# Dealing two small experts' 23 steps out by weight instead of one behind every four units

## The chip, the cores and the metric

The kernel runs on one core of a Trainium2 chip. The metric is the device time of one execution in microseconds (us). TensorE (PE) multiplies, VectorE (DVE), ScalarE (ACT) and GpSimd (POOL) do elementwise work, and SyncE (SP) issues most of the transfers from HBM. Weights come from HBM into on-chip buffers, and matmul results land in eight PSUM banks.

## The reference, cut to what matters

Two trunk layers run on 384 tokens (128 context tokens and 256 latent tokens). Layer 0 ends in a dense SwiGLU, layer 1 in a mixture of eight SwiGLU experts, of which each token takes two. Only the mixture is touched by the change:

```python
def _swiglu(x, wg, wu, wd):
    return (jax.nn.silu(x @ wg) * (x @ wu)) @ wd

def _moe(h, router, wg, wu, wd):          # D = 1024, D_FF_EXPERT = 1792, 8 experts
    logits = (xt @ router).astype(jnp.float32)
    top_v, top_i = lax.top_k(logits, TOP_K)
    gates = jax.nn.softmax(top_v, axis=-1)
    ...
    for e in range(N_EXPERTS):
        y = y + combine[:, e:e + 1] * _swiglu(xt, wg[e], wu[e], wd[e])
```

All weights are float32: an expert's three matrices are 22 MB, so all eight are 176 MB, read once.

## The kernel before

**Positions.** The kernel sorts six of the experts by how many tokens chose them (experts 0 and 1 keep their places) and works through *positions* 0 to 5 one after the other, with 128 token slots each (`expert`, L1440). Position 2 (`BIG`) has 32 extra slots. The two smallest experts are positions 6 and 7 (`PAIR`), with 64 slots each. They have no turn of their own: their work is cut into 23 *steps* that are woven in behind the units of positions 1 to 5.

**Units.** A position has 23 units, each one transfer of two 128-row slabs: four for the first half of the gate matrix (`mg`), four for the first half of the up matrix (`mu`), four and four for the second halves, seven for the down matrix (`md`). A unit of `mg` or `mu` is 896 KB, a unit of `md` 1024 KB. `Stream` (L50) loads the units in a fixed order (`woven_units`, L198) through SP into *slots*: five in the tile `raw`, and whole tiles lent at times (`O`, which the trace calls Z, `V` and `lnb`). A load waits until the unit that held its slot is done with it. A unit of positions 0 to 5 is split by ACT (`hi`, a rounded copy) and DVE (`lo`, the rest), both at L129, in two parts per unit and a ring of four parts; its slot is free after the split. PE then does three products per part (L1324 for `mg` and `mu`, L1471 for `md`): 12 matmuls a unit.

**The extra slots of position 2.** They are multiplied unsplit, by the raw weights in full float32, behind every second unit (L1333, L1491). Slots of position 2 are therefore kept until those matmuls are done.

**A step of the pair** (`products`, L1345) takes one unit of expert 6 and one of expert 7, both raw, in 16 matmul instructions that use one half of the array's columns each (L1352): two slots, 1.8 or 2.1 MB. The results of a group of steps (four for each half of `mg` and `mu`, seven for `md`) collect in two held PSUM banks. What ends a group (a silu on ACT or a product on DVE, L1378 and L1380) is issued at the next call of the generator `pair_work`. The 24th call, behind the last step, is the *tail*: two gate products (`slot_gate`), then L1395 to L1398, which read the two banks of the pair's `md` group.

**Where the steps lie.** `weave` (L1403) is called behind every unit of positions 1 to 5 and counts them; behind every fourth (`EVERY`) it takes one step of the pair. `woven_units` puts the pair's two loads behind the same unit of the load order. So steps 1 to 5 lie in position 1, 6 to 11 in position 2, 12 to 17 in position 3, 18 to 23 in position 4, and the tail behind the fourth unit of position 5.

**What sets the order.** PSUM banks are handed out in turn by `bank` (L237), skipping held ones, in the order in which the code asks. The order in each engine's queue is chosen when the program is built, by a planner that follows its own estimate of when operands are there. It need not be that of the code. `behind_last` (L106) ties side work on ACT and DVE behind the split that was issued last. `turn_act` (L1416) transposes an expert's activations on PE, and ACT and DVE copy them (L1423, L1424); `chores` are six DVE operations on 128x1024 and one ACT operation, one behind each of the first units of position 1. `gather_pair` collects the tokens for two positions, in the `md` units of positions 1 and 3.

Of the kernel before, what the change touches and what calls it, by code (L numbers as in the profile page):

```python
# [40 lines left out]
BIG = 2  # L41
# [1 line left out]

NA = 6
PAIR = (6, 7)
EVERY = 4
LATE = 4


class Stream:  # L50
# [20 lines left out]
    def add(self, key, src, nk, n, split=True):  # L71
        i = len(self.units)
        self.units.append((key, src, nk, n, split))
        self.first[i] = len(self.parts)
        if split:
            step = PART // n
            self.parts += [(i, k, min(step, nk - k), n) for k in range(0, nk, step)]
# [56 lines left out]
    def next(self, key):  # L134
        while callable(self.units[self.at][1]):
            self.at += 1
        i = self.at
        assert self.units[i][0] == key, (self.units[i][0], key)
        self.at += 1
        return i  # L140
# [44 lines left out]
def moe_units(key, add, ins, e):  # L185

    def of(name, *at):
        ap = ins[name]
        return ap[(e, *at)]
    for h in range(2):  # L190
        for name in ("mg", "mu"):
            for u in range(4):
                add((name, key, h, u), of(f"w_{name}", h, u), 2, HFE)
    for u in range(NFE // 2):
        add(("md", key, u), of("w_md", u), 2, D)


def woven_units(add, ins, experts, pair):  # L198

    both = []  # L200
    for key, e in pair:
        both.append([])
        moe_units(key, lambda *a: both[-1].append(a), ins, e)
    both = list(zip(*both))
    at = [0]

    def one(*a):
        add(*a)
        at[0] += 1
        if at[0] % EVERY == 0 and both:  # L210
            for u in both.pop(0):
                add(*u, False)

    for key, e in experts:
        moe_units(key, one, ins, e)
    assert not both
# [11 lines left out]
def kernel(ctx: ExitStack, tc: tile.TileContext, ins, outs):  # L228
# [320 lines left out]
    def some(chores, n=1):  # L549

        for _ in range(min(n, len(chores))):
            with st.behind_last():
                chores.pop(0)()
# [557 lines left out]
    def moe(l, cq, ck, h2, O, V):  # L1111
        with tc.tile_pool(name="moe", bufs=1) as mp, tc.tile_pool(name="spill", bufs=1, space=bass.MemoryType.DRAM) as dp:
# [39 lines left out]
            big, at, cap = (S[:, 192 + 8 * i:200 + 8 * i] for i in range(3))  # L1152
# [161 lines left out]
            def half(w, e, h, name, c, po):  # L1314
                open_ = [bank(hold=True) for _ in range(2)]
                ps = [x[:, 0:448] for x, _ in open_]
                whole = []
                for u in range(4):
                    key = (name, e, h, u)
                    for k, _, wh, wl in w.split(key):  # L1320
                        kk = 2 * u + k
                        for s, m, first, last in ((xH, wh, kk == 0, False), (xH, wl, False, False), (xL, wh, False, kk == NK - 1)):
                            for i in range(2):
                                pe.matmul(ps[i], s[:, kk, c], m[:, 0, 448 * i:448 * i + 448], start=first, stop=last)  # L1324
                    if po is not None:

                        whole.append((u, *w.raw(key)))
                    for v, i, x in whole if u % 2 else ():
                        for k in range(2):
                            kk = 2 * v + k  # L1330
                            for j in range(4):
                                a = min(256 * j, HFE - 256)
                                pe.matmul(po[32 * j:32 * j + 32, :], xo[:, kk, :], x[:, k, a:a + 256],  # L1333
                                          start=kk == 0, stop=kk == NK - 1)
                        w.release(i)
                    if u % 2:
                        whole.clear()
                    weave(w, e)
                for _, x in open_:
                    held.discard(x)  # L1340
                return ps
# [59 lines left out]
            woven = [0, 0]  # L1401

            def weave(w, e):  # L1403

                if w is st and e:
                    some(chores)
                    if e == LATE:
                        woven[1] += 1
                        with st.behind_last():
                            for f in under.get(woven[1], ()):  # L1410
                                f()
                    woven[0] += 1
                    if woven[0] % EVERY == 0:
                        next(pair, None)

            def turn_act(h):  # L1416
# [23 lines left out]
            def expert(w, e, c, extra=False, between=None, after=None):  # L1440
# [25 lines left out]
                for u in range(NFE // 2):  # L1466
# [31 lines left out]
                    if u == 4 and after:  # L1498
                        with tc.issue_after(m.ins) if e == NA - 1 else ExitStack():
                            after()  # L1500
                    weave(w, e)
                summed(pd, e)
                if extra:
# [337 lines left out]
```

## Time and profile before

| | us |
|---|---|
| median of 3 runs (lowest, highest) | 1224.32 (1219.56, 1224.40) |
| the profiled execution, its own time | 1222.04 |
| its span, first to last instruction | 1220.3 |
| position 1, from its first matmul to that of position 2 | 732.2 to 825.6 |
| position 2 | 825.6 to 933.4 |
| position 3 | 933.4 to 1028.0 |
| position 4 | 1028.0 to 1124.9 |
| position 5 and the last sums on PE | 1124.9 to 1202.3 |

The trace is of one execution. All times in the rows below are microseconds from the span's start unless a column says ns. "PEclk" is the clock that TensorE was granted, as a share of 2.4 GHz; "DMA share" is the mean busy share of the 16 transfer engines. "PE busy" includes the modelled ends of pipelined matmuls, so a busy PE can still be slowed: lost time shows in the idle time in brackets, in the granted clock, and in matmuls that take longer than others of the same form. A window's line is its start and end, its length, then the busy time (instructions) of PE, PEld, DVE, ACT and POOL, the mean PEclk, the DMA share and GB/s; where it is of one line of the kernel, PE and PEld alone.

### The profile page before, as it was taken

What the parts mean: (1) busy time and instruction counts of PE and PEld (TensorE: products, weight loads), DVE (VectorE), ACT (ScalarE), POOL (GpSimd) and SP (SyncE); (2) the same over time, 40 slices, a digit from 0 to 9 for tenths busy, and PEclk for the clock granted to TensorE, in tenths of its full rate; (3) what the DMA queues carried; (4) which work ended last, traced back from release to release, by engine and by line L of the source; (5) the groups of instructions that cost most, each with busy time, mean ns of one, the idle gap of its engine ahead of it and who ended that gap; (6) DMA issues with size and microseconds to landing.
All of it is one profiled execution on the core that took longest, in us unless ns stands there. A gap on an engine that the chain in (4) does not pass through costs nothing.

```text
span 1220.3 us, 16646 instructions
## 1 busy us (share of the span) xinstructions
PE 1167.0 (96%) x6216; PEld 921.4 (76%) x6216; DVE 814.9 (67%) x1306; ACT 589.1 (48%) x871; POOL 73.5 (6%) x106
## 2 busy tenths in 40 slices
PE   7999999999999998999999999999999999999894
PEld 5877686999999877888786886776666767666782
DVE  3665646888885436577657988575565657668895
ACT  3534526323232334454636866455444536556771
POOL 0110000000000000010000700000000000110002
PEclk9999998999999999899999999999999999999997
DMA  9877327566653241645143888969889997999961
GB/s 370 342 254 276 138 105 280 203 242 226 240 223 139 104 151 59 246 164 204 36 155 133 328 354 303 386 257 340 310 297 349 376 364 290 413 401 396 355 264 55
DMA packets 50647, 308.98 MB, mean 253 GB/s; under 512 B 5768, under 2 KB 8456, under 8 KB 30208
## 3 DMA queue, kind: packets, MB, share of 16 engines
q1 hardware_dynamic: 46672, 294.58, 63.0%
q0 software_dynamic: 2576, 10.20, 2.3%
q10 hardware_dynamic: 1312, 3.07, 0.7%
q8 instruction: 51, 0.84, 0.3%
q14 instruction: 36, 0.29, 0.1%
HBM read 303.66 MB, written 4.17 MB: 252 GB/s over the span
## 4 chain that ended last, share of the span: by engine, by line
PE 80%; issue 6%; DVE 6%; DMA 4%; ACT 2%; POOL 1%; SPq 0%; ACTq 0%; POOLq 0%; DVEq 0%
PE bank L1324 13%; PE bank L950 12%; PE bank L340 10%; PE bank L342 9%; PE bank L341 9%; PE bank L1471 8%; PE bank L1352 5%; DVE lo L129 3%; PE bank L382 2%; DMA raw<-in_w_mg_dram 2%; PE bank L1333 1%; DMA raw<-in_w_mod_dram 1%; ACT hi L129 1%; PE bank L883 1%; PE bank L1175 1%
## 5 line engine op out<-in xcount | busy, mean ns | idle before, releaser
L129 DVE TENSOR_TENSOR lo<-raw,hi 128x1024 fp32r<-128x1024 f32 (+3 forms) x330 | 369.3, 1141 | 186.6 <-ACT hi L129 183.0
L129 ACT CAST hi<-raw 128x1024 fp32r<-128x1024 f32 (+3 forms) x330 | 318.9, 986 | 294.4 <-PE bank L341 75.3
L340 PE MATMUL bank<-actH,hi 128*128 128x384 f32 x352 | 119.2, 339 | 2.9 <-ACT actH L499 2.9
L1324 PE MATMUL bank<-hi,actH 128*128 128x448 f32 x384 | 114.0, 378 | 6.6 <-DVE V L1395 4.8
L341 PE MATMUL bank<-actL,hi 128*128 128x384 f32 x352 | 119.2, 339 | 0.0
L342 PE MATMUL bank<-actH,lo 128*128 128x384 f32 x352 | 118.8, 337 | 0.0
L1324 PE MATMUL bank<-lo,actH 128*128 128x448 f32 x384 | 112.9, 375 | 2.9 <-DVE lo L129 2.9
L1324 PE MATMUL bank<-hi,actL 128*128 128x448 f32 x384 | 110.3, 369 | 0.0
L1324 PEld LDWEIGHTS bank<-hi,actH 128*128 128x128 f32 x384 | 71.0, 191 | 27.5 <-issue 13.4
L1324 PEld LDWEIGHTS bank<-lo,actH 128*128 128x128 f32 x384 | 70.9, 190 | 18.9 <-DVE lo L129 8.8
L1324 PEld LDWEIGHTS bank<-hi,actL 128*128 128x128 f32 x384 | 72.8, 189 | 6.0
L340 PE MATMUL bank<-hi,actH 128*128 128x512 f32 (+2 forms) x192 | 71.3, 373 | 3.1 <-ACT gT L495 2.5
L950 PE MATMUL bank<-hi,gs 128*128 128x512 f32 x264 | 73.0, 390 | 0.0
L340 PEld LDWEIGHTS bank<-actH,hi 128*128 128x128 f32 x352 | 66.9, 190 | 7.1 <-ACT actH L499 3.7
L341 PE MATMUL bank<-lo,actH 128*128 128x512 f32 (+2 forms) x192 | 69.3, 361 | 0.5 <-DVE lo L129 0.5
L342 PE MATMUL bank<-hi,actL 128*128 128x512 f32 (+2 forms) x192 | 67.4, 360 | 0.0
L341 PEld LDWEIGHTS bank<-actL,hi 128*128 128x128 f32 x352 | 66.9, 190 | 0.2 <-DVE actL L500 0.2
L342 PEld LDWEIGHTS bank<-actH,lo 128*128 128x128 f32 x352 | 67.0, 190 | 0.0
L1471 PE MATMUL bank<-hi,maH 128*128 128x512 f32 x168 | 56.2, 404 | 3.9 <-ACT hi L129 3.9
L1471 PE MATMUL bank<-lo,maH 128*128 128x512 f32 x168 | 56.2, 401 | 2.0 <-DVE lo L129 2.0
L950 PEld LDWEIGHTS bank<-hi,gs 128*128 128x128 f32 x264 | 49.4, 188 | 11.0 <-ACT gs L1038 0.9
L1471 PE MATMUL bank<-hi,maL 128*128 128x512 f32 x168 | 54.6, 394 | 0.0
(488 smaller groups left out, 2018.1 us busy)
## 6 DMA issues: line engine op xcount, KB each, us to landing
raw<-in_w_mg_dram SPq DMA_DIRECT2D x53, 896.0 KB, 7.2
raw<-in_w_mu_dram SPq DMA_DIRECT2D x48, 896.0 KB, 7.7
raw<-in_w_md_dram SPq DMA_DIRECT2D x40, 1024.0 KB, 7.3
raw<-in_w_mod_dram SPq DMA_DIRECT2D x39, 1024.0 KB, 4.9
lnb<-in_w_md_dram SPq DMA_DIRECT2D x11, 1024.0 KB, 9.2
raw<-in_w_fg_dram SPq DMA_DIRECT2D x10, 1024.0 KB, 6.5
raw<-in_w_fu_dram SPq DMA_DIRECT2D x10, 1024.0 KB, 4.9
raw<-in_w_fd_dram SPq DMA_DIRECT2D x10, 1024.0 KB, 4.8
```

Source lines behind the costliest of these rows:

```text
L129: self.last = nc.scalar.copy(hi, raw), nc.vector.tensor_sub(lo, raw, hi.bitcast(F32))
L340: pe.matmul(out, sh, mh, start=first, stop=False)
L341: pe.matmul(out, sh, ml, start=False, stop=False)
L342: pe.matmul(out, sl, mh, start=False, stop=last)
L382: pe.matmul(pb[32 * j:32 * j + 32, :], condS[:, 2 * u + kp, :], w[:, kp, 512 * h:512 * h + 512], start=u == 0, stop=u == 3)
L883: pe.matmul(po[:, 0:256], vK[:, 1 + j, c], pT_[:, h % 2, j, :], start=j == 0, stop=j == 2)
L950: r = pe.matmul(hold[2 * b + h][0], s[:, k, c], m[:, 0, 512 * h:512 * h + 512], start=f, stop=z)
L1175: pe.matmul(o, h[b][:, c], Pm[:, b, 0:n], start=j + b == 0, stop=j + b == NB)
L1324: pe.matmul(ps[i], s[:, kk, c], m[:, 0, 448 * i:448 * i + 448], start=first, stop=last)
L1333: pe.matmul(po[32 * j:32 * j + 32, :], xo[:, kk, :], x[:, k, a:a + 256], start=kk == 0, stop=kk == NK - 1)
L1352: pe.matmul(ps[i][0][r, 0:n], s[kk + k][:, r], x[:, k, n * i:n * i + n], start=first, stop=last)
L1471: r = pe.matmul(pd[i][0], s[:, kk, :], m[:, 0, 512 * i:512 * i + 512], start=first, stop=last)
```

## The change

The count that deals out the steps goes up by 3 behind a unit of position 2 and by 1 behind any other, and a step is taken each time it reaches 6; `woven_units` counts the same way for the loads. So a step comes behind every second unit of position 2 and every sixth unit of the others. No instruction is added or removed, and the 23 steps and the tail keep their order.

```diff
-EVERY = 4
+EVERY, HEAVY = 6, 3
...
     def one(*a):
         add(*a)
-        at[0] += 1
-        if at[0] % EVERY == 0 and both:
+        at[0] += HEAVY if a[0][1] == BIG else 1
+        if at[0] >= EVERY and both:
+            at[0] -= EVERY
             for u in both.pop(0):
                 add(*u, False)
...
-                    woven[0] += 1
-                    if woven[0] % EVERY == 0:
+                    woven[0] += HEAVY if e == BIG else 1
+                    if woven[0] >= EVERY:
+                        woven[0] -= EVERY
                         next(pair, None)
```

| steps in position | 1 | 2 | 3 | 4 | 5 |
|---|---|---|---|---|---|
| before | 5 | 6 | 6 | 6 | tail, behind its unit 4 |
| after | 3 | 12 | 4 | 4 | tail, behind its unit 6 |

## Rows read from the trace of the kernel before

**Rows 1.** The page: the chain that ended last; the split's two groups (busy, mean ns).
```profile
PE 80%; issue 6%; DVE 6%; DMA 4%; ACT 2%; POOL 1%; SPq 0%; ACTq 0%; POOLq 0%; DVEq 0%
...
L129 DVE TENSOR_TENSOR lo<-raw,hi 128x1024 fp32r<-128x1024 f32 (+3 forms) x330 | 369.3, 1141 | 186.6 <-ACT hi L129 183.0
L129 ACT CAST hi<-raw 128x1024 fp32r<-128x1024 f32 (+3 forms) x330 | 318.9, 986 | 294.4 <-PE bank L341 75.3
```
**Rows 2.** Windows, positions 1, 2, 4, then part of 3; columns as named below.
```profile
732.20:825.60 93.40, 90.55 (x419) 65.47 (x418) 66.68 (x85) 52.22 (x67) 0.00 (x0) 0.98 0.82 317
825.60:933.40 107.80, 107.80 (x766) 70.22 (x764) 59.47 (x73) 51.90 (x65) 0.00 (x0) 1.00 0.86 314
...
1028.00:1124.90 96.90, 94.64 (x410) 60.95 (x410) 67.36 (x69) 52.19 (x63) 8.24 (x6) 1.00 0.99 400
...
952.00:965.70 13.70, 13.70 (x73) 10.60 (x72) 9.83 (x11) 7.34 (x10) 0.00 (x0) 1.00 1.02 425
```
**Rows 3.** The chain in order: start, us, what (units, steps, extra slots).
```profile
777.76 9.72 PE bank L1324 x48
787.48 3.16 PE bank L1352 x16
...
836.62 5.06 PE bank L1324 x24
841.68 1.86 PE bank L1333 x32
...
1039.38 3.58 PE bank L1352 x16
```
**Rows 4.** Windows of L1352 alone: positions 1, 2, 4, then two whole steps.
```profile
732.20:825.60 93.40, 20.64 (x80) 5.80 (x80) 0.98 0.82 317
825.60:933.40 107.80, 19.37 (x96) 6.36 (x96) 1.00 0.86 314
...
1028.00:1124.90 96.90, 30.47 (x112) 8.67 (x112) 1.00 0.99 400
846.10:849.30 3.20, 3.19 (x16) 1.06 (x16) 1.00 0.92 348
1071.30:1075.00 3.70, 3.66 (x16) 1.11 (x16) 1.00 1.03 424
```
**Rows 5.** PE and ACT timelines where PE stood still in positions 1 and 3.
```profile
793.23 0.73 PE L1471 MATMUL bank<-hi,maH 128*128 128x512 f32 x2 [1.67 <-ACT hi L129]
794.62 1.07 PE L1471 MATMUL bank<-lo,maH 128*128 128x512 f32 x2 [0.66 <-DVE lo L129]
...
791.27 0.97 ACT L1423 CAST maH<-bank 128x512 fp32r<-128x512 f32 x2 [7.67 <-PE bank L1421]
...
970.58 0.68 PE L1324 MATMUL bank<-hi,actH 128*128 128x448 f32 x2 [1.41 <-ACT hi L129]
971.71 0.67 PE L1324 MATMUL bank<-lo,actH 128*128 128x448 f32 x2 [0.45 <-DVE lo L129]
```
**Rows 6.** PE and DVE timelines around the tail, in position 5.
```profile
1139.70 1.25 PE L1324 MATMUL bank<-hi,actH 128*128 128x448 f32 x2 [4.84 <-DVE V L1395]
...
1137.55 1.41 DVE L1535 SCALAR_TENSOR_TENSOR V<-Z,cst,V 128x512 f32<-128x512 f32 x2
1138.87 1.28 DVE L1395 TENSOR_TENSOR V<-bank,V 128x512 f32<-128x512 f32 x2
1141.07 1.29 DVE L1398 TENSOR_TENSOR mE<-V,mE 128x512 fp32r<-128x512 f32 x2
```
**Rows 7.** Window around the lower clock behind the first stop (position 1).
```profile
794.50:798.50 4.00, 3.88 (x10) 3.06 (x11) 4.00 (x9) 2.57 (x3) 0.00 (x0) 0.57 0.39 129
```
**Rows 8.** What PE waited for in position 4: us in total, times, longest.
```profile
PE bank L1324 <- DVE lo L129: 1.5, 3, 0.6
```
**Rows 9.** Issue to landing of L88's loads, in position 2, then 4.
```profile
DMA to landing us min/median/max: 4.5/6.0/8.7
...
DMA to landing us min/median/max: 6.9/10.2/13.0
```

## The prediction

> **What bounds the kernel now.** I read the page first, to see which engine the end hangs on: PE holds 80% of the chain that ended last [rows 1]. No edit here takes work off PE, so only time that PE loses can be won. Next come the windows by position, where the reader should compare two columns: PE's busy time against the length, and the rate of the transfers [rows 2]. In position 2 PE is busy for all of 107.8 us while transfers run at 314 GB/s; in position 4 they run at 400 GB/s with the transfer engines busy 0.99 of the time, and PE is idle for 2.3 us. A stretch of position 3 shows 425 GB/s, the highest rate that I found, which I take as the ceiling. So the mixture is bound by PE, with transfers just behind it everywhere but in position 2.
>
> Third, the chain in order gives the price of each piece [rows 3]: four units take 9.72 us (2.43 each), a step of the pair 3.16 us for mg or mu and 3.58 for md, two units of position 2 take 5.06 and their extra slots 1.86. From these and the sizes (896 KB is 0.918 MB, 1024 KB is 1.049 MB) comes the rate that each pattern asks for:
>
> - four units and a step (position 3 before): 9.72 + 3.16 = 12.88 us for 6 x 0.918 = 5.51 MB, 428 GB/s; with md steps (position 4) 13.30 us for 5.77 MB, 434.
> - six units and a step (positions 1, 3, after): 14.58 + 3.16 = 17.74 us for 7.34 MB, 414 GB/s; with md steps 18.16 us for 7.60 MB, 419.
> - position 2 before, four units, twice the extra slots, a step: 17.0 us for 5.51 MB, 324 GB/s. After, two units, the extra slots, a step: 5.06 + 1.86 + 3.16 = 10.08 us for 3.67 MB, 364 GB/s.
>
> Before, positions 1, 3 and 4 ask for a little more than the ceiling and position 2 for far less; after, all are under it.
>
> Fourth, the timelines show where PE lost time. In position 1 it stood 1.67 and 0.66 us, in position 3 1.41 and 0.45 [rows 5], in position 5 4.84 [rows 6]. Behind each of the three lies a window of 4 us with a mean granted clock of 0.57 (the first is shown), which is 3.4 us at 1.2 GHz instead of 2.4 [rows 7]: half of 3.4, 1.7 us, is lost on top. So the stops cost 4.0, 3.6 and 6.5 us. Position 4 adds 1.5 us of waits for the split [rows 8]. Last, steps that were torn apart: a step's 16 matmuls run in pairs, one expert in each half of the array's columns, if they stand together. A whole step keeps PE busy for 3.19 us, one of md for 3.66; five in position 1 should be 15.9 us and are 20.64, seven md steps in position 4 (the 17th ran there) 25.6 and are 30.47 [rows 4]. That is 4.7 and 4.9 us lost; the six of position 2 lose 0.2. All that can be won is thus about 4.0 + 3.6 + 6.5 + 1.5 + 9.6 = 25 us.
>
> **The change part by part.** PE's work is the same and so are the bytes; six steps (19 us, 11 MB) leave positions 1, 3 and 4, two each, for position 2.
>
> *The tail.* PE's stop of 4.84 us ends with DVE's L1395 [rows 6]. Counting `bank` calls through the code says why: the mu group of position 5 opens behind unit 4 and is handed the two banks of the pair's md group, which the tail, issued at that very point, has still to read. Counted again with the new dealing, the tail comes behind unit 6; the mu group has by then got two banks that position 4 left, and the pair's banks go to the mg group behind unit 8, two units (4.9 us) later. The wait has its cover. What stays is DVE's own work in the tail, 1.41 + 1.28 + 1.29 = 4.0 us, ahead of splits that PE needs. The ring has three parts ahead (3 x 1.22 us), of which a part's own split uses 0.99 + 1.14 = 2.1 [rows 1], so some 1.5 us are hidden and 2.5 show; the lower clock may or may not follow. I take 3.0 us left of 6.5, so 3.5 won; bounds 6.5 and 0.
>
> *The stops in positions 1 and 3.* Both follow a step that stands just ahead of a transposition [rows 5]: ACT waits 7.67 us for PE's transposes behind the step (L1423), with the next split queued behind it on ACT. In position 1 the step came behind its last mu unit; after the change no step of position 1 stands there. But in position 3 one does now, and another stands behind the second unit of the second mg half, where the second stop was. Without a change of cause I would expect as many stops as before; with fewer bytes asked for there, fewer. Of 7.6 us I take 3 won; bounds 7.6 won and 1 lost.
>
> *Torn steps.* The order comes from the build's planner, which fills PE with half a step when a split is not there yet by its reckoning. The torn steps lie in positions 1 and 4, 0.8 us a step over 12 steps. With 3 and 4 steps there, 7 x 0.8 = 5.6 remain, 4.0 won. Position 2 tore none when it asked for 324 GB/s; at 364 it stands nearer to 324 than to 428, but not at it: I take 2 us lost there, between 0 and 12 x 0.8 = 9.6. Net 2.0 won.
>
> *Waits for the split in position 4* were 1.5 us at 434 GB/s; at 419 I take 1.0 won, between 0 and 1.5.
>
> *Position 2's slots.* Its slots are kept until the extra matmuls, and a step takes two more. There are seven (five, Z, lnb). In a cycle of 10.08 us that begins with the first unit, the two units free theirs at 6.0 and 6.9 us and the step at 10.1; a load takes the slot of the unit seven ahead of it. The second unit of the next cycle but one is thus issued at 10.1 us and used at 22.7, less 2.1 for its split: 10.5 us from issue to landing, the tightest of the four (the others have 11 or more). Landing takes 6.0 us in the median there now and 8.7 at most; in position 4 10.2 and 13.0 [rows 9]. 364 GB/s lies between, so the cover should hold. I take 1 us lost.
>
> The Trainium skill speaks against this change at one place: "DMA: Bandwidth & Descriptors", section "Where 436 GB/s comes from", puts the bound of transfers from HBM at about 358 GB/s for a core. By that, position 2's new cycle would take 3.67 MB / 358 = 10.25 us in place of 10.08, 2 us more over 12 steps, and the sum would end at 1215.5. The trace disagrees, with 425 GB/s over 13.7 us [rows 2].
>
> *Covered at no cost:* the silu and products that end a group of the pair (four operations on 448 columns, by L1395's 0.64 us each 2.6 us [rows 6], all beside PE's work) move with the steps; where they share banks with the next group, as before in position 1, the planner has a unit to run in between.
>
> Sum, against the profiled execution's 1222.0: less 3.5, 3, 2.0 and 1.0, plus 1, gives 1213.5. That execution lies 2.3 us under the median of the runs shown, inside their spread; I predict 1213.5.
>
> **The rivals.**
>
> *The stops and torn steps move along with the steps.* The planner tears and misplaces by its own clock, not by the chip's, so position 2 would get what the others lose. For it: the same two places of position 3 again; 414 GB/s is only 3% under 428. Against it: position 2 had neither at six steps. Only the tail is won: 1222.0 - 3.5 = 1218.5.
>
> *Position 2 tears its steps as 1 and 4 did*, 9.6 us instead of 2: 1213.5 + 7.6 = 1221. For it: 364 GB/s again and again for 115 us, with two raw units due at once. Against it: six steps there lost 0.2 us [rows 4].
>
> *Position 2 runs out of slots* (the slower side). From 10.5 us issue to landing on, each of the 12 cycles waits for a load. At position 4's longest, 13.0 us, a cycle lacks 2.5 us, of which its own stretching gives back a tenth: 12 x 2.3 = 27, 1213.5 - 1 + 27 = 1239.5. It is slower than before from 11.4 us on. For it: slots are held longest in position 2, and landing there is 4.5 us at best [rows 9]. Against it: it was 8.7 us at most, and the rate asked stays 14% under the ceiling.
>
> *The planner's order hardly follows the dealing*, and stops and waits are as before: 1222. For it: position 4 ran seven steps where the code has six. Against it: position 2 ran the six that the code has there, all but whole [rows 4].
>
> **How the numbers follow.** Forecast 0.45; stops and tears move along 0.22; torn steps in position 2 0.18; slots 0.08; no effect 0.07. The range must leave out no more than 2 in 10: from 1203 (stops and tears mostly gone) to 1228, which takes in all cases but the slots and the worst sums. A measurement of this kernel can tell about 0.5% (6 us) from no change. Faster by more (under 1216): 0.41 of the forecast, 0.06 of the second case, 0.03 of the third, together 0.50. Slower (over 1228): 0.07 of the slots, 0.05 of worse sums, 0.12. Within: 0.38.
>
> **What would show it.** Right: position 5's mu group opens with no wait for L1395, and the lower clock behind it is gone; position 2 lasts 107.8 + 6 x 3.2 = 127 us with PE busy throughout and about 355 GB/s; positions 1, 3 and 4 are shorter by more than two steps each (6.4, 6.4, 7.2 us). Wrong: PE waiting on hi or lo in position 2 with landings over 10.5 us (slots); L1352 over 3.2 us a step there (torn); a stop at the start of position 3's md units with the clock at 0.5 behind it (moved along).

## The result, and the profile after

| | before | after |
|---|---|---|
| median (lowest, highest), us | 1222.38 (1219.1, 1224.4), 6 runs | 1228.5 (1227.22, 1230.31), 6 runs |
| profiled execution, its span | 1222.04, 1220.3 | 1228.41, 1226.6 |
| position 1 (steps in it) | 93.4 (5) | 82.9 (3) |
| position 2 | 107.8 (6) | 137.3 (12) |
| position 3 | 94.6 (5) | 98.8 (4) |
| position 4 | 96.9 (7) | 84.6 (4) |
| position 5, to the last sums | 72.1 | 69.0 |

The change made the kernel slower: ratio 1.0058, 95% interval 1.0044 to 1.0072, 6.1 us. 1213.5 was predicted.

The windows of after by position, with the columns of [rows 2]:

```profile
730.70:813.60 82.90, 82.28 (x388) 62.28 (x386) 66.92 (x85) 52.02 (x65) 0.00 (x0) 1.00 0.88 330
813.60:950.90 137.30, 137.30 (x862) 76.75 (x860) 57.76 (x72) 52.64 (x70) 2.04 (x4) 1.00 0.78 310
950.90:1049.70 98.80, 91.36 (x446) 69.09 (x445) 60.87 (x71) 52.43 (x68) 1.11 (x2) 0.97 0.83 330
1049.70:1134.30 84.60, 78.35 (x355) 58.43 (x353) 65.59 (x67) 51.33 (x61) 9.23 (x6) 0.96 0.99 395
1134.30:1203.30 69.00, 67.02 (x316) 57.36 (x315) 57.83 (x62) 47.99 (x58) 0.00 (x0) 1.00 0.73 285
```

Read it with the steps in hand, at 3.19 us for a whole step and 3.66 for one of md [rows 4]. Position 1 gave up two steps (6.4 us) and is 10.5 us shorter: 4.1 more than they weigh. Position 4 gave up three of md (11.0) and is 12.3 shorter, 1.3 more. Position 5 is 3.1 shorter, and the mixture starts 1.5 us earlier. Against that, position 2 took six steps (19.1 us) and is 29.5 longer: 10.4 too many. Position 3 went from five steps of mg or mu to one and three of md, 1.8 us less work, and is 4.2 longer: 6.0 too many. In sum 10.4 + 6.0 - 4.1 - 1.3 - 3.1 - 1.5 = 6.4, and the spans differ by 6.3; the rest is rounding. So two positions hold the whole loss, and they lose in different ways: in position 2 PE is busy for all of 137.3 us at full clock, with transfers at only 310 GB/s; in position 3 it stands idle for 7.4 us and the mean clock is 0.97.

**Position 2: the extra slots' groups are torn.** The extra slots' matmuls of the `mg` and `mu` units alone (L1333 before, L1334 after), in position 2 (length, PE busy, PEld busy), before and then after:

```profile
825.60:933.40 107.80, 17.92 (x256) 7.96 (x256) 1.00 0.86 314
```
```profile
813.60:950.90 137.30, 22.22 (x256) 8.37 (x256) 1.00 0.78 310
```

The same 256 matmuls keep PE busy 4.3 us longer; eight whole groups of 1.86 us [rows 3] would be 14.9. Counted along PE's timelines, the eight groups of 32 ran in 12 pieces before and run in 21 after. A part of the timeline of after shows how (start, duration, instruction, count):

```profile
829.61 0.68 PE L1325 MATMUL bank<-hi,actH 128*128 128x448 f32 x2
830.21 1.05 PE L1334 MATMUL bank<-raw,mod 128*32 128x256 f32 x10
831.19 0.67 PE L1325 MATMUL bank<-lo,actH 128*128 128x448 f32 x2
...
833.42 1.50 PE L1334 MATMUL bank<-raw,mod 128*32 128x256 f32 x22
834.84 0.47 PE L1325 MATMUL bank<-hi,actH 128*128 128x448 f32 x1
```

A group of 32 is run as 10 and 22, with matmuls of a main unit between them. From start to next start the pieces take 0.98 and 1.42 us, 2.40 for what takes 1.86 whole. The matmuls of a group use a quarter of the array's columns each (the form 128*32) and overlap when they stand together: 32 of them, each recorded with some 0.38 us, take 1.86 us. That every piece has to begin and end this overlap anew fits the times, but the trace shows only the times.

**Position 3: a wait on ACT for a transfer.** ACT's timeline, PE's, and the window of the lower clock:

```profile
1019.62 1.05 ACT L129 CAST hi<-raw 128x1024 fp32r<-128x1024 f32 x1 [0.33 <-PE bank L1473]
1030.63 1.33 ACT L1536 ACTIVATE mod<-Z,cst 128x512 f32<-128x512 f32 x2 [9.95 <-DMA Z<-gate]
1031.87 1.98 ACT L129 CAST hi<-raw 128x1024 fp32r<-128x1024 f32 x2
1033.75 2.03 ACT L1180 CAST actH<-bank 128x512 fp32r<-128x512 f32 x4
```
```profile
1035.95 1.04 PE L1218 MATMUL bank<-cst,actH 128*64 128x1 f32 x12 [5.31 <-DVE actL L1181]
```
```profile
1035.20:1042.20 7.00, 6.25 (x29) 5.43 (x30) 2.91 (x7) 3.23 (x7) 0.00 (x0) 0.51 0.39 131
```

`slot_gate` for position 4 (L1536) waits on ACT until a row of gates has been spread to all partitions by a transfer. Behind it on ACT stand the casts of the next units and those of the tokens gathered for position 4 (L1180). PE runs out of work, stands 5.31 us, and then runs for about 7 us at 0.51 of the clock. Transfers stop as well (2 GB/s between 1030.6 and 1035.2 us), because slots come free only by the split.

**Position 4** now has two stops and low clock behind them, where before it had 1.5 us of short waits [rows 8]. ACT, then PE:

```profile
1069.32 1.15 ACT L1565 ACTIVATE mE<-mE,cst 128x1024 f32<-128x1024 f32 x1 [4.34 <-DMA mE<-yb,rowof]
```
```profile
1071.34 0.68 PE L1325 MATMUL bank<-hi,actH 128*128 128x448 f32 x2 [1.80 <-ACT hi L129]
1075.19 1.11 PE L1325 MATMUL bank<-lo,actH 128*128 128x448 f32 x2 [3.17 <-DVE lo L129]
```

The chain of work that ended last, in order (start, us, what), runs through exactly these transfers: the spread of the gates, then the write of the experts' rows to memory and the fetch from there.

```profile
1019.69 10.87 DMA Z<-gate
...
1050.68 9.72 DMA yb<-mE
...
1062.62 10.13 DMA mE<-yb,rowof
```

**Position 5.** Of PE's 4.84 us and the low clock behind them [rows 6] these are left, at full clock:

```profile
1154.68 0.67 PE L1325 MATMUL bank<-lo,actH 128*128 128x448 f32 x2 [0.53 <-DVE lo L129]
1156.88 0.68 PE L1325 MATMUL bank<-lo,actH 128*128 128x448 f32 x2 [1.12 <-DVE lo L129]
```

### The profile page after: what moved, and what is told of

The parts are those of the page before. It is cut to its first block, busy times and chain, and to the rows that moved or that the text cites. A ratio compares the mean times of both kernels' runs of the same rounds, so it can differ in the third digit from the quotient of the medians.

```text
span 1226.6 us, 16643 instructions
## 1 busy us (share of the span) xinstructions
PE 1172.2 (96%) x6216; PEld 921.3 (75%) x6216; DVE 813.2 (66%) x1306; ACT 588.2 (48%) x871; POOL 73.6 (6%) x106
## 5 line engine op out<-in xcount | busy, mean ns | idle before, releaser
L129 DVE TENSOR_TENSOR lo<-raw,hi 128x1024 fp32r<-128x1024 f32 (+2 forms) x318 | 356.1, 1144 | 176.7 <-ACT hi L129 174.2
L129 ACT CAST hi<-raw 128x1024 fp32r<-128x1024 f32 (+2 forms) x318 | 307.3, 988 | 253.3 <-PE bank L342 74.4
L1325 PEld LDWEIGHTS bank<-lo,actH 128*128 128x128 f32 x384 | 70.3, 189 | 26.4 <-DVE lo L129 14.5
L951 PE MATMUL bank<-hi,gs 128*128 128x512 f32 x264 | 72.9, 390 | 0.0
L129 DVE TENSOR_TENSOR lo<-lnb,hi 128x896 fp32r<-128x896 f32 (+1 forms) x40 | 44.0, 1127 | 25.9 <-ACT hi L129 24.4
```

The lines of the kernel that those rows point to most:

```text
L129: self.last = nc.scalar.copy(hi, raw), nc.vector.tensor_sub(lo, raw, hi.bitcast(F32))
L951: r = pe.matmul(hold[2 * b + h][0], s[:, k, c], m[:, 0, 512 * h:512 * h + 512], start=f, stop=z)
```

## The experiments

The theory after the traces: (1) in position 2 the planner tears the groups of extra slots more than before, now that a step comes with every group; (2) in positions 3 and 4 two ACT operations that wait for transfers (`slot_gate` and the join) stand ahead of the casts; they were placed by unit counts, and the steps that used to pass between issue and use have moved away. The rivals: position 2 is short of transfers or slots; the pair's own steps are torn, as the prediction had it; position 4 is short of transfers (0.99 of the engines' time busy), so that its stops cost nothing; the new dealing is worth nothing by itself. Each kernel is given with its ratio to the kernel before, measured beside it on the same chip (its median there: 1221.67 us for e1 to e4, 1222.7 for e5 to e8, 1222.34 for e9 and e10).

**e1: order tied in position 2.** Main units, extra-slot groups and steps each follow the last matmul of the one before, in the code's order.

```diff
+            def whole_block(e, w):
+                if w is st and e == BIG:
+                    seen = []
+                    with tc.issue_after(pin[0].ins) if pin[0] else ExitStack():
+                        yield seen
+                    pin[0] = seen[-1]
...
-                        for k in range(2):
-                            kk = 2 * v + k
+                        with whole_block(e, w) as seen:
+                            for k in range(2):
+                                kk = 2 * v + k
...
```

> The new dealing, with PE's order in position 2 tied to that of the code (main unit, extra slots, step, each whole); nothing else changed. Theory A (the planner's torn order is the loss): position 2 lasted 137.4 us where 107.8 + 6 x 3.2 = 127 was due, because the extra slots' matmuls and steps were torn; whole, position 2 takes 127 to 129 us and the kernel 8 to 10 us less, 1219 to 1221. Theory B (the splits or loads are not there in time, and the torn pieces only fill time that PE would stand idle): PE idles in position 2 for what it gains, position 2 stays at 135 us or more, and the kernel within 2 us of 1228.5.

Measured 1213.98 (1212.89 to 1216.61), ratio 0.994 (0.9921 to 0.9959): 14.5 us less than after, more than expected. Position 2 is 125.9 us, and still PE is never idle there:

```profile
812.80:938.70 125.90, 125.90 (x862) 75.97 (x860) 59.16 (x73) 53.44 (x70) 1.73 (x4) 1.00 0.88 341
```

Transfers rose from 310 to 341 GB/s when PE asked for more. So neither transfers nor slots limited position 2. Worked out from start to next start of PE's instructions, by line: the extra slots (those of `md` included) fell from 29.8 to 22.2 us, the steps from 39.9 to 37.9, the main units from 64.8 to 62.9. These are also the three places where the change had lost: in the kernel before, the same lines took 23.7, 19.0 (for six steps; twelve whole ones are 37.9) and 62.4 us. Of the rest of the gain, in the profiled executions, 0.8 us lies ahead of position 2 and some 2.3 behind it (position 3 is 1.9 shorter).

**e2: slot_gate tied.** In the changed kernel, the operation that waits for the gates goes behind the split that was issued last.

```diff
                 if e == LATE:
-                    slot_gate(W6, W6, cs[:, 0:2])
+                    with st.behind_last():
+                        slot_gate(W6, W6, cs[:, 0:2])
```

> The new dealing, with the gate product of position 4 (slot_gate for W6, two operations each on ACT and DVE) tied behind the split that was issued last, so that ACT does not wait for the gate's transfer ahead of position 3's splits. Theory A (that wait, 10 us on ACT, makes the 5.3 us stop of PE in position 3, empties the load queue and so makes the stops of 1.8 and 3.2 us in position 4, each with the clock at half behind it): all three go, 10 to 15 us less, 1213 to 1218. Theory B (the loads are short there anyway): the stops come back at other places, less than 4 us gained.

Measured 1221.06 (1220.1 to 1224.46), ratio 0.9997 (0.9986 to 1.0008): 7.4 us less than after. ACT's gathered tokens no longer wait for the transfer, and the stop of 5.31 us is gone:

```profile
1026.99 0.59 ACT L1180 CAST actH<-bank 128x512 fp32r<-128x512 f32 x1 [2.86 <-PE bank L1176]
...
1061.64 1.15 ACT L1565 ACTIVATE mE<-mE,cst 128x1024 f32<-128x1024 f32 x1 [3.51 <-DMA mE<-yb,rowof]
```

Position 3 is 91.1 us, 7.7 less. The profiled execution is one of the longer ones of e2 (1223.97 us): there positions 4 and 5 give 1.7 and 1.6 us back. The expectation was wrong in its second half: I had put position 4's stops down to the same delay, but they stayed (PE stands 1.77 and 3.17 us). The second row shows why: the join still waits for its fetch.

**e3: both together.**

> The new dealing with both edits of e1_order2 and e2_gate. Theory A: the gains add, 18 to 24 us less than the changed kernel, 1205 to 1210, under the kernel before by 12 us or more. Theory B: no faster than the kernel before.

Measured 1211.37 (1210.21 to 1212.49), ratio 0.9914 (0.9898 to 0.9931): 17.1 us less than after, of 21.9 by e1 and e2 alone. Position 3 had got 1.9 of its 7.7 already in e1. Position 4's stops are again there (84.9 us).

**e4: slot_gate tied in the kernel before.** The same edit as e2.

> The kernel before with the gate product tied as in e2_gate. There ACT waited 9.3 us for the gate's transfer too, and PE 2.2 us. If that wait is a loss of both kernels: 2 to 4 us less than before, 1218 to 1220. If it is a loss that only the new dealing has: within 1 us of before.

Measured 1218.76 (1217.69 to 1220.95), ratio 0.9972 (0.9961 to 0.9982), position 3 2.4 us shorter. The wait was there before the change, and nearly as long; ACT's timeline of the kernel before:

```profile
1006.27 0.72 ACT L1534 ACTIVATE mod<-Z,cst 128x512 f32<-128x512 f32 x1 [9.27 <-DMA Z<-gate]
```

It ended 72.9 us into position 3, against 79.7 after the change. From issue to landing the spread, a transfer of 1024 KB, took 5.1 us before and 10.9 us after. What the loads' queue moved beside it in these times (packets, MB, share of the engines), before and then after:

```profile
q1 hardware_dynamic: 35, 0.16, 7.4%
```
```profile
q1 hardware_dynamic: 417, 2.79, 65.8%
```

Tying the wait was worth 2.4 us of position 3 there, and 7.7 after the change.

**e5: e3, and the joins one unit later.** Experts' rows are fetched behind unit 2 of position 4 and joined from unit 5 on; here from unit 6 on.

```diff
-                    under.setdefault(5 + 6 * b + i, []).append(partial(joined, b, i))
+                    under.setdefault(6 + 6 * b + i, []).append(partial(joined, b, i))
```

> e3_order2_gate with the joins of position 4 (L1565 and what follows: ACT and DVE read what GpSimd's indirect load fetched) one unit later each, six units behind the fetch's count of two instead of five. In e3_order2_gate ACT waited 4.0 us for that fetch, and PE stood 1.4 and 3.1 us behind it with the clock at half. Theory A (the join, dealt out by units, came too early once no step lay between fetch and join): the stop goes, 5 to 7 us less than e3_order2_gate, 1204 to 1207. Theory B (position 4 is short of transfers, at 0.98 to 1.03 of the engines busy, and would stop anyway): within 2 us of 1211.

Measured 1208.76 (1206.6 to 1210.4), ratio 0.9889 (0.9868 to 0.991): 2.6 us less than e3, between the two expectations, and the two intervals overlap. PE's longest stop in position 4 is 2.34 us in place of 3.09, with no low clock behind it. But position 4 is no shorter for it (e3, then e5):

```profile
1032.40:1117.20 84.80, 78.20 (x355) 57.80 (x353) 66.88 (x69) 52.12 (x63) 9.21 (x6) 0.98 0.99 399
```
```profile
1031.00:1115.70 84.70, 79.51 (x355) 56.18 (x353) 67.13 (x69) 52.37 (x63) 9.90 (x6) 1.00 0.98 399
```

The two profiled executions differ by 1.4 us, and the mixture starts 1.6 us earlier in e5. So e5 does not show that the joins cost time in the new dealing, and the rival stays open there: transfers run at 399 GB/s in both, with the engines busy 0.98 of the time or more. The join still waits, ACT for 1.50 us and DVE for 3.93, so one unit is not all the cover that it needs. In the kernel before a step lay between fetch and join; the new dealing took it away.

**e6: the kernel before with the tail behind unit 6 of position 5,** and nothing else.

```diff
-                    if woven[0] % EVERY == 0:
+                    if woven[0] % EVERY == 0 and woven[0] < 96 or woven[0] == 98:
```

> The kernel before with one part of the change alone: the tail behind unit 6 of position 5 instead of unit 4, by calling the 24th step there; every step stays where it was. Theory A (PE's stop of 4.84 us was the wait for the pair's two banks): the wait for L1395 is gone, 3.5 to 5 us less than before, 1217 to 1218. Theory B (DVE's 4 us of the tail stop PE wherever they lie): within 1.5 us of before.

Measured 1218.47 (1213.89 to 1219.56), ratio 0.9961 (0.9944 to 0.9979). Position 5 is 68.9 us, as after the change, with no wait for L1395; waits of 0.78 and 1.14 us for `lo` are left. So the tail's place alone is worth the 3.1 us of position 5, as the prediction had it.

**e7: the kernel before with the order tied in positions 1 to 5, and slot_gate tied.** The edits of e1 (for all positions) and e2.

> The kernel before (a step behind every fourth unit) with the gate tied as in e4_before_gate and PE's order in positions 1 to 5 tied to the code's, so that no step and no extra-slot group is torn. Theory A (torn steps are lost time, 4.7 us in position 1 and 4.9 in position 4): 7 to 10 us less than e4_before_gate, 1209 to 1212, and then the new dealing itself is worth little once the order is tied (e3_order2_gate: 1211). Theory B (the torn pieces filled time in which splits were not there): within 3 us of e4_before_gate, 1216 to 1220, and the new dealing is worth 5 us or more.

Measured 1216.59 (1215.31 to 1219.81), ratio 0.9953 (0.9934 to 0.9971). The second expectation holds. Whole steps and groups shorten position 1 by 4.4 us and position 2 by 2.4, but PE has two new stops, 2.70 us at the end of position 1 and 3.36 us at the end of position 3: a step that has to keep its place waits until the two banks of its group are read (e10 below shows the same two in its rows). Position 4 loses 3.9 us (97.2 with six steps, 96.9 with seven before), and there ACT waits for the fetch of the join as it does after the change:

```profile
1045.53 1.15 ACT L1583 ACTIVATE mE<-mE,cst 128x1024 f32<-128x1024 f32 x1 [3.82 <-DMA mE<-yb,rowof]
```
```profile
1024.70:1121.80 97.10, 88.98 (x394) 60.38 (x392) 67.73 (x69) 53.63 (x65) 9.05 (x6) 0.95 0.97 387
```

The two new stops suggest that some of the tearing was the planner's way around waits.

**e8: the changed kernel with all of it:** order tied in positions 1 to 5, slot_gate tied, joins a unit later.

> The new dealing with gate and joins as in e5_order2_gate_join and PE's order tied in all positions instead of position 2 alone. Theory A (torn steps of position 1, 13.6 us for three, are lost time): 3 to 4 us less than e5_order2_gate_join. Theory B (in position 1 the six chores on DVE, 7.3 us, hold the splits up, and the pieces filled that): within 1.5 us of e5_order2_gate_join.

Measured **1203.7** (1203.31 to 1206.02), ratio 0.9856 (0.9837 to 0.9875): the best version, 18.7 us under the kernel before and 24.8 under the changed one. It is 5.1 us under e5, and position 1 alone gives 4.9 of that, so the first expectation holds. Its windows by position:

```profile
730.90:809.10 78.20, 76.89 (x388) 62.23 (x387) 65.53 (x85) 51.46 (x65) 0.00 (x0) 1.00 0.90 350
809.10:935.00 125.90, 125.90 (x863) 75.96 (x861) 59.62 (x74) 53.71 (x70) 2.03 (x4) 1.00 0.88 339
935.00:1025.10 90.10, 88.28 (x447) 66.86 (x446) 58.55 (x67) 51.06 (x64) 1.10 (x2) 1.00 0.88 357
1025.10:1109.90 84.80, 78.49 (x356) 56.15 (x354) 67.27 (x69) 52.51 (x63) 9.88 (x6) 1.00 0.98 399
1109.90:1178.80 68.90, 66.66 (x317) 57.37 (x316) 57.76 (x62) 47.94 (x58) 0.00 (x0) 1.00 0.73 283
```

Full clock in every position. What is left is in position 4, where PE is idle for 6.3 us.

**e9: only the extra slots and the main units of position 2 tied,** the pair's steps free. It is e1 without the tie of the steps, and tells the torn groups from the torn steps.

```diff
-                    with whole_block(at_e[0], st) as seen:
+                    with whole_block(0, st) as seen:
```

> The changed kernel with only the main units and the extra-slot groups of position 2 tied to the code's order; the pair's steps stay free (one of them is then still torn). Theory A, the torn extra-slot groups are the loss of position 2: the time falls to 1214-1217 us, position 2 to 126-128 us, with the extra-slot groups at 1.9-2.0 us each. Theory B, the pair's torn steps are the loss (the rival of the prediction): the time stays above 1224 us and position 2 above 134.

Measured 1213.9 (1212.89 to 1216.6), ratio 0.9934 (0.991 to 0.9957): the whole of e1's gain. Position 2 in e9, whole and then the extra slots of `mg` and `mu` alone:

```profile
812.80:939.40 126.60, 126.60 (x862) 76.01 (x860) 58.22 (x73) 52.78 (x70) 0.65 (x2) 1.00 0.85 336
```
```profile
812.80:939.40 126.60, 16.29 (x256) 7.50 (x256) 1.00 0.85 336
```

The 256 matmuls are back at 16.29 us from 22.22; seven of the eight groups are whole and one still runs in three pieces. A whole group in e9's PE timeline:

```profile
831.43 1.93 PE L1348 MATMUL bank<-raw,mod 128*32 128x256 f32 x32
```

Two limits of this experiment: the main units are tied with the groups, so the split between these two (7.6 and 1.9 us in e1) rests on the sums by line alone. And with both held in order there were fewer places left to tear a step, and only one of the twelve was torn. So it shows that the order of groups and main units was nearly the whole loss of position 2, and not that free steps never are.

**e10: the old dealing with all of the remedies,** the tail behind unit 6 included.

> The kernel before, old dealing, with the same remedies as the best version (order tied in positions 1 to 5, slot_gate and joins tied a unit later) and the tail behind unit 6. Theory A, the new dealing itself is worth something even when all that hung on the unit counts is mended, because positions 1, 3 and 4 no longer wait for their loads: 1208-1212 us, 4 to 8 us above the changed kernel with these remedies (1203.7). Theory B, the dealing's gain was the tail and the waits alone: within 2 us of 1203.7.

Measured 1209.56 (1208.82 to 1211.45), ratio 0.9897 (0.987 to 0.9924): 5.9 us above e8, so the first expectation holds. Its windows, positions 1 to 4, and two of PE's stops:

```profile
729.80:818.90 89.10, 83.76 (x420) 64.90 (x419) 66.23 (x85) 52.92 (x68) 0.00 (x0) 1.00 0.90 347
818.90:924.30 105.40, 105.06 (x766) 69.86 (x764) 60.06 (x73) 51.98 (x65) 0.00 (x0) 1.00 0.82 308
924.30:1024.30 100.00, 94.74 (x474) 69.45 (x471) 58.85 (x68) 51.23 (x66) 3.14 (x6) 0.97 0.88 350
1024.30:1116.40 92.10, 87.45 (x395) 58.59 (x393) 67.40 (x69) 52.98 (x65) 8.43 (x6) 1.00 1.00 406
```
```profile
807.34 0.59 PE L1367 MATMUL bank<-raw,cst 128*64 128x448 f32 x1 [2.70 <-ACT V L1393]
...
1016.12 0.64 PE L1367 MATMUL bank<-lnb,V 128*64 128x512 f32 x1 [3.36 <-DVE V L1395]
```

By position against e8, with the work of the steps that differ: 10.9 us longer in position 1 for 6.4 of work, 9.9 in position 3 for 5.4, 7.3 in position 4 for 7.3, and 20.5 shorter in position 2 for 19.1. So beyond the work it loses 4.5 in positions 1 and 3 each, nothing in position 4, and wins 1.4 in position 2: 7.6 us over the five positions, of which a start 1.1 us earlier gives back some (the profiled executions differ by 6.6). The new dealing by itself is worth 5.9 us with these remedies, and it earns that in positions 1 and 3, by stops that it avoids. The two stops above, 6.1 us, come from the tie, which makes a step wait for the banks of the group before; whether the old dealing with an order that avoids them would be as fast as e8 is open.

Against e7, e10 differs by the joins and the tail alone, and the tail lies behind position 4. Position 4 is 5.0 us shorter, ACT and DVE no longer wait for the fetch, and transfers run at 406 GB/s in place of 387. So in the old dealing the joins' wait does cost time; in the new dealing e5 did not show it.

## Why the prediction was wrong

**The step that failed first: "Position 2 tore none when it asked for 324 GB/s".** I had looked at the pair's steps alone (L1352) [rows 4]. The line beside it, L1333, held 17.92 us before, where whole groups would be 14.9: position 2 did tear before the change, in the extra slots, not in the steps. The term was set at 2 us lost, with 9.6 as its far end; position 2 lost 10.4. By start to next start, 1.9 of that lies in the steps, which is near the 2 us of the term; 6.1 lies in the extra slots and 2.4 in the main units, and these two were no term at all. (Tying the order won 7.6 in the extra slots, more than the change had lost there, because some of their groups had been torn before it.) The rival "position 2 tears its steps" had the right place and nearly the right sum, 9.6 us, with the wrong instruction in it: that its sum came near is luck.

**The step that failed second: the stops in positions 1 and 3, "7.6 won and 1 lost" at the ends.** For position 1 it was right: no stop is left there, and 4.1 us beyond the steps were won. In position 3 the stop moved to the start of the `md` units, as said (1.29 and 0.52 us, with no low clock behind them). But `slot_gate`'s wait on ACT was not among the steps that the prediction priced. It stood in the kernel before, for 9.27 us, at a cost of 2.4 us by e4, and I had not looked at what else of ACT's queue waits for a transfer. With it position 3 lost 6.0.

**The step that failed third: the waits of position 4, "1.0 won, between 0 and 1.5".** The row that was priced grew from 1.5 to 4.1 us, and all of PE's idle time in position 4 from 2.3 to 6.3; in PE's waits of after, position 4 (us in total, times, longest):

```profile
PE bank L1325 <- DVE lo L129: 4.1, 3, 3.2
PE bank L1325 <- ACT hi L129: 1.8, 1, 1.8
```

The prediction reckoned them by the rate of transfers, 419 for 434 GB/s. The two long stops lie behind the join, which waits for its fetch; the distance between the two is counted in units and so became a step shorter. In the old dealing a longer distance made position 4 5.0 us shorter (e7 and e10). What the stops cost in the new dealing stays open: with four steps, position 4 takes 84.0 to 86.3 us in every run, whatever was tied, at 393 GB/s or more. The Trainium skill's figure of about 358 GB/s for a core ("DMA: Bandwidth & Descriptors", "Where 436 GB/s comes from") binds none of these rows; all of them are of one core at work.

**What was right.** The tail: 3.5 us forecast, 3.1 found in position 5 and again in e6, with no wait for the product of the tail. Position 2's slots: PE never idle, 1 us forecast and none found, although landings reached 12.4 us where 10.5 had been put as the edge (issue to landing, position 2):

```profile
DMA to landing us min/median/max: 4.4/7.5/12.4
```

The edge was worked out for the tightest unit at 10.08 us a cycle, and torn groups stretch the cycle in after; in e8, where position 2 lasts about as long as forecast, no landing took over 8.5 us. Position 2's whole length, forecast at 127 us and PE busy throughout, is that of e1 and e8 (125.9).

**Torn steps in positions 1 and 4: the sum right, the parts not.** The pair's steps (L1353) in positions 1 and 4 of after (length, PE busy, PEld busy):

```profile
730.70:813.60 82.90, 14.41 (x48) 3.55 (x48) 1.00 0.88 330
...
1049.70:1134.30 84.60, 14.53 (x64) 4.33 (x64) 0.96 0.99 395
```

4.0 us were to be won by 0.8 a step. Position 4 tears none any more (14.53 / 4 = 3.63), 4.9 won. Position 1 loses as much as before, 14.41 - 3 x 3.19 = 4.8, on three steps instead of five: the tearing does not go by the step. e8 takes it away (position 1 4.7 us shorter than in e1).

**The rivals.** "Stops and tears move along with the steps" was nearest in its kind: position 4 lost its torn steps and position 2 got torn pieces, in a line that I had not counted. The ends were set from what rows showed of the steps, and 1228.5 lies 0.5 us beyond them.

## What to carry to other kernels

When work is dealt out anew, list everything that is placed by a count of units (a join three units behind its fetch, an operation at an expert's border) and every operation on a split engine that waits for a transfer: the distance that covers it is in time, and changes with the dealing. When a build chooses the order by its own estimates, look for torn groups in every packed line, not only in the one that is moved: divide a line's busy time by the number of its groups and compare with one whole group. And tie the order before judging a new dealing: here the same dealing is 0.6% slower than the kernel before as the build orders it, and 1.4% faster with the order, the gates and the joins tied (the old dealing with these remedies and the tail moved: 1.0%).

## What the runs showed of the hardware

Cutting a packed group costs time that no single instruction shows. The groups of position 2 (busy us, mean ns of one, idle before), of after and then of e9:

```profile
L1334 PE MATMUL bank<-raw,mod 128*32 128x256 f32 x160 | 14.6, 386 | 0.0
```
```profile
L1348 PE MATMUL bank<-raw,mod 128*32 128x256 f32 x160 | 10.7, 383 | 0.0
```

An extra-slot matmul takes 386 ns torn and 383 ns whole in the mean, yet 160 of them keep PE busy for 14.6 or 10.7 us. From the lines' starts, an extra piece costs about 0.5 us (2.40 against 1.86 for one cut into two). The Trainium skill, "TensorEngine Tiling (Array Packing)", section "Key Properties", says that changing the tiling mode drains TensorE. The trace agrees in direction, with 0.5 us for one more change there and back; how much of that is the drain no run here separates.

A transfer of 1024 KB, the spread of the gates, took 5.1 us from issue to landing where 0.16 MB of loads moved beside it, and 10.9 us where 2.79 MB did.

The granted clock fell to 1.2 GHz behind PE's stops of 5.31 us in position 3 and of 1.80 and 3.17 us in position 4, and not behind 1.29 and 0.52 us in position 3. Two windows of after, from within the stop of 3.17 us on and behind that of 1.29, in the columns of [rows 2]:

```profile
1072.80:1079.60 6.80, 4.41 (x12) 3.94 (x13) 6.75 (x7) 2.23 (x4) 1.55 (x1) 0.50 0.87 343
1007.65:1019.70 12.05, 11.52 (x53) 8.50 (x54) 11.23 (x17) 9.54 (x13) 0.53 (x2) 1.00 0.69 273
```

In the kernel before, 1.67 and 0.66 us had been followed by the lower clock [rows 5, 7]; 2.77 us in e8's position 4 and 2.70 us in e10's position 1 were not (1.00 over the 7 us from each stop's end on). The length of one stop alone does not tell.
